# The first x of a batched matmul: eight-row transfers for three of its row tiles, plain transfers for the fourth

## The chip, the cores and the metric

The kernel runs on one core of a Trainium2 chip. The core has five engines that run at their own pace: TensorE (PE) multiplies and transposes, VectorE (DVE) and ScalarE (ACT) copy results out of PE's accumulators, GpSimd (POOL) and SyncE (SP) here only issue transfers. Sixteen DMA engines move data between the chip's memory (HBM) and the core's on-chip memory (SBUF, 128 partitions). Each issuing engine has its own queue to these sixteen: the profile calls POOL's queue q0 and SP's q1.

The metric is device time in microseconds (us); it was 514.31 as the median of three runs (514.30 to 514.31). A profile of one further execution shows what every engine and every DMA packet did.

## The reference

```python
batch, m, k, n = 32, 512, 1024, 768
"x": np.random.randn(batch, m, k).astype(np.float32)
"weight": np.random.randn(batch, k, n).astype(np.float32)

def reference(x, weight):
    return np.matmul(x, weight).astype(np.float32)
```

These are 32 independent products of 512x1024 by 1024x768. All inputs and outputs are 32-bit floats in HBM: 67 MB of x, 101 MB of weights, 50 MB of results.

## The kernel before

Each batch is cut into four row tiles of 128 rows (MT = 4) and eight slices of the contraction (KT = 8). Row tile mt holds the rows 4p + mt of x, p being the partition, so that a partition's four rows lie side by side in HBM, 16 KB in all.

**Loads.** Weights come a batch at a time (`load_w`, line 70), x two batches at a time (`load_pair`, line 60), both from POOL's queue, which turns 32-bit floats into bf16 on the way. Four weight buffers (w_pool) and three x buffers (x_pool) are in use; a load waits on POOL until PE has finished with the buffer that it takes. POOL works its list strictly in order: the weights of batch 0, the identity matrix for the transposes, x of batches 1 and 2, weights 1 and 2, x of 3 and 4, then in the loop weights three batches ahead, x four batches ahead and the stores of finished pairs (`store`, line 164), except the last ones.

**The first x** is the exception. It is loaded by SP as 32-bit floats, which needs no conversion: three of its row tiles go to `x_first` (line 151: one transfer of 128 partitions with 12 KB each) and the fourth to `x_fourth` (line 154: 17 transfers). These 17 are 32, 16, 16, 2 and 2 rows of 4 KB, and then twelve of five rows each, rows of every fourth partition within blocks of twenty. SP keeps eight transfers under way, so each further one waits until an earlier one has landed. SP's list ends with the last stores (lines 182, 184, 185 and 215).

**Compute.** PE must have x with the contraction on the partitions, so it transposes each row tile against an identity matrix, into PSUM (`pt`), and DVE copies it to `xT` in bf16. Line 105 does this for the first x (`transpose_first`), line 78 for the others. The matmuls of line 123 add up eight slices into three accumulators (`pm`) for two row tiles at a time; ACT and DVE copy them to `outs` (lines 143 to 145). For batch 0 three row tiles are transposed before the first matmul, and the fourth when its turn comes (line 211).

**Order.** The program is written in a manual schedule: each engine does its instructions in the order of the source. For batch 0 PE's order is: 24 transposes of `x_first`, the 48 matmuls of the first three row tiles, 8 transposes of `x_fourth`, its 16 matmuls, and then the transposes of batches 1 and 2.

Of the kernel before, what the change touches and what calls it, by code (L numbers as in the profile page):

```python
# [13 lines left out]
def kernel(  # L14
# [6 lines left out]
    nc = tc.nc  # L21
    B, M, K = x.shape
    _, _, N = weight.shape
    P = 128
    MT = M // P
# [21 lines left out]
    x_view = x.rearrange("b (mi mo) k -> b mi mo k", mi=P)  # L47
# [6 lines left out]
    def banks():  # L54
        return [mpsum.tile([P, 512], F32, name=f"pm{i}") for i in range(3)]

    def load_pair(b):

        xs[b] = x_pool.tile([P, 2 * MT, K], BF16, name="x_sb")
        nc.gpsimd.dma_start(out=xs[b], in_=pair_view[b // 2])  # L60

    def load_last():
        xs[B - 1] = x_pool.tile([P, MT, K], BF16, name="x_sb")
        nc.gpsimd.dma_start(out=xs[B - 1], in_=x_view[B - 1])  # L64

    def load_w(b):
        ws[b] = w_pool.tile([P, KT, N], BF16, name="w_sb")
        at = 0
        for n in CHUNKED.get(b, (KT,)):
            nc.gpsimd.dma_start(out=ws[b][:, at:at + n, :], in_=w_view[b, :, at:at + n, :])  # L70
            at += n
# [9 lines left out]
    def transpose_pair(b, mt):  # L81

        both = xT_pool.tile([P, 2, JT, P // 2, 2, 2], BF16, name="xT")
        for half in range(2):
            nc.vector.tensor_copy(  # L85
                both[:, :, :, :, half, :].rearrange("p b j i r -> p j b i r"),
                words(b, mt + MT * half).rearrange("p j (b i r) -> p j b i r", b=2, r=2),
            )
        return [both[:, r].rearrange("p j i h r -> p j (i h) r") for r in range(2)]

    def transpose_last(mt):
        xT = xT_pool.tile([P, JT, P, 2], BF16, name="xT")
        nc.vector.tensor_copy(  # L93
            xT.rearrange("p j m r -> p (j m r)"), words(B - 1, mt).rearrange("p j m -> p (j m)")
        )
        return xT

    def transpose_first(mt):

        xT = xT_pool.tile([P, JT, P, 2], BF16, name="xT")  # L100
        rows = x_first[:, mt] if mt < MT - 1 else x_fourth[:, 0]
        for h in range(2):
            pt = tpsum.tile([P, JT, P], F32, name="pt")
            for i in range(JT):
                nc.tensor.transpose(pt[:, i, :], rows[:, JT * h + i::KT], ident)  # L105
            nc.vector.tensor_copy(  # L106
                xT[:, 2 * h:2 * h + 2].rearrange("p j m r -> p j r m"),
                pt.rearrange("p (j r) m -> p j r m", r=2),
            )
        return xT  # L110
# [8 lines left out]
    def matmuls(pm, half, xT, b, kos, together):  # L119
        for ko in kos:  # L120
            for i, (bank, at, off, size) in enumerate(SPLITS[half]):
                shares = half == 1 and i == 0
                nc.tensor.matmul(  # L123
                    pm[bank][:, at:at + size],
                    xT[:, ko // 2, :, ko % 2],
                    ws[b][:, ko, off:off + size],
                    start=(ko == 0 and not (together and shares)),
                    stop=(ko == KT - 1),
                    skip_group_check=together,
                )  # L130

    def open_out(b):

        if b == B - 2:
            outs[b] = one_pool.tile([P, MT * N], F32, name="one_sb")
            return
        if b % 2 == 0 or b == B - 1:
            twos[b // 2] = out_pool.tile([P, 2, MT * N], F32, name="out_sb")
        outs[b] = twos[b // 2][:, b % 2]

    def evacuate(b, pair, pm):
        o = outs[b][:, pair * N2:(pair + 1) * N2]
        nc.scalar.copy(o[:, 0:512], pm[0])  # L143
        nc.vector.tensor_copy(o[:, 512:1024], pm[1])  # L144
        nc.scalar.copy(o[:, 1024:N2], pm[2])  # L145

    with tc.manual_schedule():

        x_first = x_pool.tile([P, MT - 1, K], F32, name="x_sb")
        x_fourth = one_pool.tile([P, 1, K], F32, name="one_sb")  # L150
        nc.sync.dma_start(x_first, x_view[0, :, :MT - 1])  # L151
        few = [slice(at, first + 20, 4) for first in (0, 20, 40) for at in range(first, first + 4)]
        for rows in (slice(64, 96), slice(96, 112), slice(112, P), slice(60, 62), slice(62, 64), *few):
            nc.sync.dma_start(x_fourth[rows, 0], x_view[0, rows, MT - 1])
        load_w(0)
        ident = const.tile([P, P], F32)
        make_identity(nc, ident)
        load_pair(1)
        load_w(1)
        load_w(2)  # L160
        load_pair(3)

        def store(at):
            nc.gpsimd.dma_start(out=two_view[at], in_=twos[at])  # L164

        ready = {}
        for b in range(B):
            if b % 2 and b + AHEAD + 1 < B:
                if b + AHEAD + 1 == B - 1:
                    load_last()  # L170
                else:
                    load_pair(b + AHEAD + 1)
            if b % 2 and 2 < b < B - HELD - AHEAD:
                store((b - 3) // 2)
            if b + AHEAD < B:
                load_w(b + AHEAD)
            if b == B - LATE:
                store(b // 2 - 2)
                store(b // 2 - 1)
            if b == B - 1:  # L180
                halves = [slice(pair * N2, (pair + 1) * N2) for pair in range(2)]
                nc.sync.dma_start(out_view[b - 1, :, halves[0]], outs[b - 1][:, halves[0]])
                for late in range(B - LATE, B - 2):
                    nc.sync.dma_start(out_view[late], outs[late])
                nc.sync.dma_start(out_view[b - 1, :, halves[1]], outs[b - 1][:, halves[1]])
            open_out(b)
            if b == 0:
                xT = {mt: transpose_first(mt) for mt in range(MT - 1)}
            elif b == B - 1:
                xT = {mt: transpose_last(mt) for mt in range(MT)}  # L190
            else:
                if b % 2:
                    for mt in range(MT):
                        ready[b, mt], ready[b + 1, mt] = transpose_pair(b, mt)
                xT = {mt: ready.pop((b, mt)) for mt in range(MT)}
            if b in CHUNKED:
                pms = [banks() for _ in range(2)]
                at = 0
                for n in CHUNKED[b]:
                    for mt in range(MT):  # L200
                        matmuls(pms[mt // 2], mt % 2, xT[mt], b, range(at, at + n), True)
                        if at + n == KT and mt % 2 == 1:
                            evacuate(b, mt // 2, pms[mt // 2])
                    at += n
                continue
            for pair in range(2):
                pm = banks()
                for half in range(2):
                    mt = 2 * pair + half
                    if mt not in xT:  # L210
                        xT[mt] = transpose_first(mt)
                    matmuls(pm, half, xT[mt], b, range(KT), False)
                evacuate(b, pair, pm)
                if b == B - 1:
                    nc.sync.dma_start(out_view[b, :, halves[pair]], outs[b][:, halves[pair]])
# [30 lines left out]
```

## Time and profile before

| | us |
|---|---|
| median of three runs | 514.31 |
| span of the profiled execution | 512.6 |
| PE busy (84%) | 431.9 |
| DVE busy (25%) | 130.0 |
| ACT busy (15%) | 76.2 |
| PE's first transpose starts (line 105, first three row tiles) | 10.22 |
| PE's first transpose of the fourth row tile | 42.90 |
| first matmul of batch 0 (line 123) | 15.87 |
| last store issued by SP (line 215) | 503.43 |

All times within the execution are counted from its first instruction. The profile's page gives, for each engine, its busy time; the busy share of 40 equal slices of the span as tenths; the DMA queues with their packets, megabytes and share of the 16 engines' time; and groups of equal instructions. Another view, busy time by stretches, gives the same numbers for any stretch of the span. The waits list says which engine stood idle, and whose work ended the wait. Beside these views the trace holds a record of each DMA packet: its queue, start, duration and size. It doesn't name the DMA engine that moved it. A transfer's last packet on each engine is one of 4 bytes, which counts up the semaphore that tells of its landing; so a transfer that is spread over 16 engines leaves 16 of these.

### The profile page before, as it was taken

The page shows a single profiled execution, that of the slowest core. Times are in us where ns is not written, and L with a number is a line of the kernel's source. Part 1 is how long each engine was busy: PE and PEld are TensorE (multiplying, and loading weights), DVE is VectorE, ACT ScalarE, POOL GpSimd, SP SyncE. Part 2 cuts the span into 40 slices and gives each one's busy share as a digit, 9 for nine tenths or more (in the row PEclk, how much of TensorE's full clock was granted, in tenths as well). Part 3 has the DMA queues.
Part 4 walks back from the last instruction along what each step waited for, and adds up shares of the span by engine and source line. Part 5 has one row for each costly group of instructions (what it writes and reads, how often), then busy time and mean ns, then how long its engine had stood idle before and what let it go on. Part 6 is the DMA issues. An engine that isn't in the chain of part 4 may idle for free.

```text
span 512.6 us, 5733 instructions
## 1 busy us (share of the span) xinstructions
PE 431.9 (84%) x2528; PEld 278.5 (54%) x2576; DVE 130.0 (25%) x196; ACT 76.2 (15%) x129; POOL 37.0 (7%) x69
## 2 busy tenths in 40 slices
PE   2806999999999996997979989897897979999992
PEld 1504666666666563664636546464464645666561
DVE  1203223241415140231413204151050410514130
ACT  1100121212121201111111101111111111111210
POOL 3000010101010101001010000101001000010000
PEclk9956999999999998998989979999798997999998
DMA  8999999999999999999999999999999999999998
GB/s 241 223 221 213 218 218 218 333 220 308 245 219 333 217 323 234 226 326 221 328 225 234 318 224 332 217 246 307 221 333 216 258 295 219 331 219 216 322 427 339
DMA packets 12136, 135.63 MB, mean 265 GB/s; under 512 B 1232, under 2 KB 1232, under 8 KB 2128
## 3 DMA queue, kind: packets, MB, share of 16 engines
q0 software_dynamic: 10864, 126.88, 96.5%
q1 hardware_dynamic: 1248, 8.39, 4.1%
q8 instruction: 20, 0.33, 0.2%
q14 instruction: 4, 0.03, 0.0%
HBM read 167.77 MB, written 50.33 MB: 426 GB/s over the span
## 4 chain that ended last, share of the span: by engine, by line
PE 46%; DMA 37%; issue 8%; DVE 5%; another core or an unknown queue 2%; POOL 1%; ACT 0%; SPq 0%; POOLq 0%
PE pm L123 40%; DMA w_sb<-in_weight_dram 29%; DMA one_sb<-in_x_dram 8%; PE pt L78 5%; DVE xT L85 4%; DVE out_sb L144 1%; PE pt L105 0%; POOL out_dram L164 0%; POOL x_sb L60 0%; POOL w_sb L70 0%; DVE one_sb L144 0%; DVE xT L93 0%; ACT out_sb L145 0%; SPq L151 0%
## 5 line engine op out<-in xcount | busy, mean ns | idle before, releaser
L123 PE MATMUL pm<-w_sb,xT 128*128 128x256 bf16 (+1 forms) x2000 | 349.7, 334 | 31.2 <-DMA w_sb<-in_weight_dram 28.7
L123 PEld LDWEIGHTS <-xT 128*128 128x128 bf16 x2048 | 204.6, 100 | 171.8 <-DMA w_sb<-in_weight_dram 32.2
L144 DVE COPY out_sb<-pm 128x512 f32<-128x512 f32 x62 | 42.9, 692 | 318.3 <-PE pm L123 318.3
L78 PE MATMUL pt<-ident,x_sb 128*128 128x128 f32 x496 | 79.8, 303 | 10.4 <-DVE xT L85 10.1
L78 PEld LDWEIGHTS pt<-ident,x_sb 128*128 128x128 f32 x496 | 69.3, 209 | 21.5 <-DVE xT L85 18.7
L85 DVE COPY xT<-pt 128x1024 bf16<-128x1024 bf16 x120 | 77.4, 687 | 11.0 <-PE pt L78 11.0
L143 ACT COPY out_sb<-pm 128x512 f32<-128x512 f32 x62 | 36.3, 585 | 267.4 <-PE pm L123 267.4
L145 ACT COPY out_sb<-pm 128x512 f32<-128x512 f32 x62 | 36.3, 585 | 151.1 <-PE pm L123 151.1
L70 POOL DMA_DIRECT2D w_sb<-in_weight_dram x33 | 18.0, 546 | 406.4 <-PE pm L123 405.6
L105 PE MATMUL pt<-ident,one_sb 128*128 128x128 f32 x8 | 1.9, 422 | 19.0 <-DMA one_sb<-in_x_dram 19.0
L106 DVE CAST xT<-pt 128x512 bf16<-128x512 f32 x8 | 5.9, 732 | 34.8 <-PE pt L105 34.3
L105 PE MATMUL pt<-ident,x_sb 128*128 128x128 f32 x24 | 5.8, 426 | 10.2 <-DMA x_sb<-in_x_dram 10.2
L105 PEld LDWEIGHTS pt<-ident,one_sb 128*128 128x128 f32 x8 | 1.6, 219 | 19.4 <-issue 19.4
L105 PEld LDWEIGHTS pt<-ident,x_sb 128*128 128x128 f32 x24 | 4.4, 214 | 11.2 <-issue 10.2
L164 POOL DMA_DIRECT2D out_dram<-out_sb x14 | 10.1, 719 | 0.4 <-issue 0.3
L60 POOL DMA_DIRECT2D x_sb<-in_x_dram x15 | 8.1, 539 | 11.2 <-PE pt L105 11.2
L144 DVE COPY one_sb<-pm 128x512 f32<-128x512 f32 x2 | 1.4, 692 | 9.0 <-PE pm L123 9.0
L93 DVE COPY xT<-pt 128x1024 bf16<-128x1024 bf16 x4 | 2.6, 686 | 0.2 <-PE pt L78 0.2
L145 ACT COPY one_sb<-pm 128x512 f32<-128x512 f32 x2 | 1.2, 586 | 4.2 <-PE pm L123 4.2
L143 ACT COPY one_sb<-pm 128x512 f32<-128x512 f32 x2 | 1.2, 585 | 3.8 <-PE pm L123 3.8
L143 ACT ACT_TABLE_LOAD x1 | 1.3, 1283 | 0.7 <-PEq L230 0.7
L64 POOL DMA_DIRECT2D x_sb<-in_x_dram x1 | 0.5, 536 | 0.0
(6 smaller groups left out, 0.9 us busy)
## 6 DMA issues: line engine op xcount, KB each, us to landing
w_sb<-in_weight_dram POOLq DMA_DIRECT2D x31, 1536.0 KB, 41.7
out_dram<-out_sb POOLq DMA_DIRECT2D x14, 3072.0 KB, 55.8
x_sb<-in_x_dram POOLq DMA_DIRECT2D x15, 2048.0 KB, 50.2
out_dram<-out_sb SPq DMA_DIRECT2D x2, 1536.0 KB
x_sb<-in_x_dram SPq DMA_DIRECT2D x1, 1536.0 KB
w_sb<-in_weight_dram POOLq DMA_DIRECT2D x2, 768.0 KB, 48.8
out_dram<-one_sb SPq DMA_DIRECT2D x2, 768.0 KB
out_dram<-out_sb SPq DMA_DIRECT2D x2, 768.0 KB
```

What stands on the lines that cost most here:

```text
L60: nc.gpsimd.dma_start(out=xs[b], in_=pair_view[b // 2])
L70: nc.gpsimd.dma_start(out=ws[b][:, at:at + n, :], in_=w_view[b, :, at:at + n, :])
L78: nc.tensor.transpose(pt[:, j, :], pairs[:, mo, j::JT], ident)
L85: nc.vector.tensor_copy(both[:, :, :, :, half, :].rearrange("p b j i r -> p j b i r"), words(b, mt + MT * half).rearrange("p j (b i r) -> ...
L93: nc.vector.tensor_copy(xT.rearrange("p j m r -> p (j m r)"), words(B - 1, mt).rearrange("p j m -> p (j m)"))
L105: nc.tensor.transpose(pt[:, i, :], rows[:, JT * h + i::KT], ident)
L106: nc.vector.tensor_copy(xT[:, 2 * h:2 * h + 2].rearrange("p j m r -> p j r m"), pt.rearrange("p (j r) m -> p j r m", r=2),)
L123: nc.tensor.matmul(pm[bank][:, at:at + size], xT[:, ko // 2, :, ko % 2], ws[b][:, ko, off:off + size], start=(ko == 0 and not (together an ...
L143: nc.scalar.copy(o[:, 0:512], pm[0])
L144: nc.vector.tensor_copy(o[:, 512:1024], pm[1])
L145: nc.scalar.copy(o[:, 1024:N2], pm[2])
L164: nc.gpsimd.dma_start(out=two_view[at], in_=twos[at])
```

## The change

Only the loads of the first x are changed. `x_first` comes in seven transfers: partitions 48 to 127 in one, and the partitions 0 to 47 in six of eight partitions each, every sixth partition. `x_fourth` comes in three transfers of 64, 32 and 32 partitions. The same rows go to the same places. The order on POOL, PE, DVE and ACT is the same as before; on SP 10 loads stand where 18 stood.

```diff
         x_first = x_pool.tile([P, MT - 1, K], F32, name="x_sb")
         x_fourth = one_pool.tile([P, 1, K], F32, name="one_sb")
-        nc.sync.dma_start(x_first, x_view[0, :, :MT - 1])
-        few = [slice(at, first + 20, 4) for first in (0, 20, 40) for at in range(first, first + 4)]
-        for rows in (slice(64, 96), slice(96, 112), slice(112, P), slice(60, 62), slice(62, 64), *few):
+        few = [slice(at, 48, 6) for at in range(6)]
+        for rows in (slice(48, P), *few):
+            nc.sync.dma_start(x_first[rows], x_view[0, rows, :MT - 1])
+        for rows in (slice(0, 64), slice(64, 96), slice(96, P)):
             nc.sync.dma_start(x_fourth[rows, 0], x_view[0, rows, MT - 1])
         load_w(0)
```

Line 151 of the kernel before becomes line 153 (`x_first`), line 154 becomes line 155 (`x_fourth`); the later lines move down by one.

## The prediction

> **What bounds the kernel now.** I read the slices first, then the DMA queues, then busy time by stretches, and the waits last.
>
> ```profile
> DMA  8999999999999999999999999999999999999998
> ...
> q0 software_dynamic: 10864, 126.88, 96.5%
> q1 hardware_dynamic: 1248, 8.39, 4.1%
> q8 instruction: 20, 0.33, 0.2%
> ...
> HBM read 167.77 MB, written 50.33 MB: 426 GB/s over the span
> ```
>
> The mean share of the 16 DMA engines is 90% or more in all but the first and the last slice. POOL's queue (q0) holds 96.5% of that time; SP's (q1), which alone the change touches, 4.1%. q8 matters below: 20 packets that fetch instructions.
>
> ```profile
> 6.00:48.00 42.00, 18.70 (x94) 12.43 (x95) 6.55 (x9) 1.75 (x3) 0.53 (x1) 0.76 1.03 225
> 48.00:170.00 122.00, 117.89 (x724) 78.35 (x737) 38.22 (x58) 21.06 (x36) 9.79 (x17) 1.00 1.02 254
> 170.00:424.00 254.00, 218.64 (x1260) 138.55 (x1283) 64.05 (x97) 38.04 (x65) 20.12 (x35) 0.94 1.02 265
> 424.00:504.00 80.00, 76.66 (x455) 49.17 (x462) 21.18 (x32) 14.05 (x24) 2.48 (x4) 0.97 1.02 297
> 504.00:509.00 5.00, 0.00 (x0) 0.00 (x0) 0.00 (x0) 0.00 (x0) 0.00 (x0) 0.85 0.98 409
> ```
>
> In these stretches PE's busy time stands before the first bracket, and the DMA share is the last number but one. It is 1.02 to 1.03 from 6 to 504 us (packets overlap a little at their seams) and 0.98 until 509: the DMA engines never run dry, however busy PE is. The end belongs to them too: the last store is issued at 503.43 and the last packet ends at 511.18.
>
> ```profile
> PE pt L105 <- DMA one_sb<-in_x_dram: 19.0, 1, 19.0
> ...
> PE pm L123 <- DMA w_sb<-in_weight_dram: 28.7, 9, 5.5
> ```
>
> PE waits 19.0 us at the head for the fourth row tile and 28.7 us later for weights. The chain of waits calls PE 46% of the span, but an engine that starts 19 us late and later waits 28.7 us has not set the pace. So the question is which of the 16 DMA engines has the most to do.
>
> **How far apart the engines run.** The records of the packets show it: each transfer on q0 ends in 16 packets of 4 bytes, one an engine. Their times for three transfers:
>
> ```
> x of batches 3, 4    48.38-48.91 (11 engines)   50.45-50.83 (5 engines)
> w of batch 26        420.30 420.44 420.55       421.94 ... 423.32 (13)
> out of batches 24,25 486.35 486.38 486.38       487.83 ... 489.34 (13)
> ```
>
> The five late ones at 50 us carry the twelve five-row transfers of line 154. Two of them are latest, by 2.44 us against the first: they have 14 extra packets with 14 completions, 2.44/14 = 0.174 us a pair. I followed each engine from transfer to transfer by its shift. Eight engines, none of the five, are thrown back by 0.93 to 1.13 us again and again, at the times of the 20 q8 packets, always in the same order of eight: two or three times each before the end. Three engines are neither late nor ever hit: they are the 486.35 to 486.38 above and end at 508.39, while the last ends at 511.18. The five stand at 488.03 to 488.63 by then, the eight at 487.84 to 489.34; the mean of all is 488.04. So perfect balance would be worth 489.34 - 488.04 = 1.30 us, and no more.
>
> **The change part by part.** SP's list goes from 18 loads to 10. Bytes are the same, 512 rows of 4 KB. In the records a 12 KB packet follows the one before it after 0.441 us (460 ns less 19 overlapped), a 4 KB one after 0.153.
>
> Which engines: the trace has 128, 32 and 16 rows on sixteen engines, five rows on five, two on two of these five. So I put 80 rows on sixteen (five each) and eight rows on eight, the five and three more. The other bound for the 80 is fewer engines, which I take up as a rival.
>
> - An engine outside the eight: three packets of 12 KB fewer, four of 4 KB more (eight plain rows against four): -3 x 0.441 + 4 x 0.153 = -0.71 us.
> - One of the eight: the same plus six packets of 12 KB with a completion of 0.022 each: -0.71 + 6 x 0.463 = +2.07 us against a plain engine before. The two with 14 extra pairs lose those: 2.07 - 2.44 = -0.37. The three with 12: 2.07 - 12 x 0.174 = -0.02. The three newcomers: +2.07.
> - Idle at the head: an engine outside the eight has done its five packets at about 5.2 us (the 80th packet of the trace started at 4.85), and q0's first packet starts at 5.84. In between only the fourth tile can fill it, which SP issues seventh. SP's issues take 0.25 to 0.77 us each, so it arrives 1.03 us (0.74 to 1.77, as the first load) after 3.1 to 6.2. Idle is 0 to 0.7 us; I take 0.2, as the 0.38 to 0.46 of most issues puts it at about 4.8.
> - The three newcomers are either the three that are never hit, or among the eight that are. I take the first: the five are spared as well, so five and three would be one block of eight, beside the block of eight that takes the refills in turn. No row numbers the engines; the other choice is the rival below.
>
> [...]
>
> [...] The trace's five-row transfers do fall on five engines only.
>
> Then, at the 486 to 489 us transfer: newcomers 486.38 + 2.07 = 488.45; the five at most 488.63 - 0.02 = 488.61; the eight that are hit at most 489.34 - 0.71 + 0.2 = 488.83. The last engine is 489.34 - 488.83 = 0.51 us earlier. Engines drift by up to 0.4 us from causes I can't place (the three unhit ones moved 0.65 to 1.13 over the run without a fetch), and with sixteen now close together the latest of them is more likely to be unlucky: I take 0.1 off. Sum: -0.4 us. The profiled span is 512.6 us, the median 514.31, so 1.7 lie around it and stay: 514.31 - 0.4 = 513.9.
>
> **What moves and costs nothing.** The first three tiles land later. Line 105 now starts at 10.22. On the eight, q0 and q1 take turns from 5.84 us on, one packet each, completions too, as the records show. About seven of eleven packets have started by then; three are left with four completions between seven weight packets of 0.907: 6.1 + 7 x 0.907 + 3 x 0.455 = 13.9 us. The fourth tile's eight rows and three completions then take 11 turns, mostly beside x packets of 1.208: about 26.7 us against 42.7 now, where two waits stand in SP's list and not ten. PE: 14.0 + 5.84 + 8.0 = 27.8, no wait, + 1.94 + 3.67: batch 0 done at about 33.5 instead of 48.3. PE is 15 us early, and that buys nothing: one pair of batches takes PE 26.47 us and the DMA engines 31.55 (170.67 to 423.70, eight periods), so the 15 us come back as longer waits for weights, from about 100 us on instead of 170. What hides PE is this surplus of DMA work; if it were gone, PE's tail would show whole. What waits behind the later start is POOL's load at line 60, now at 16.36, then at about 20; q0 has work until 58 by then.
>
> **Rivals.**
> The slower side: the newcomers are refill engines. Speaks for it: eleven engines are outside the five, eight of them hit. Against: the five are all spared, which a random draw of eight from sixteen seldom does. Price: 487.84 to 489.34 + 2.07 = 489.91 to 491.41, so the last is 0.6 to 2.1 us later; with three newcomers the worst is likely near the top: +1.8, 516.1. It decides once a newcomer's last transfer comes later than 489.34, from its first refills on.
>
> PE's head counts: if PE set the end, 15 us would go: about 499.5. For it: the chain's 46% PE and 19.0 us. Against: the DMA share of 1.02 through both stages, and 5.7 us from the last store's issue to the landing of a store that q1 could do alone in 8 x 0.234 = 1.9.
>
> The transfers don't spread as read: 80 rows on five engines would be 16 packets each there, 11 x 0.441 = 4.9 us more than five, on engines that take the eights as well: about 519. Nothing speaks for it but that 80 is in no row.
>
> **Numbers.** The forecast 0.66, refill engines 0.29, PE's head 0.02, no spread 0.03. About 0.2% (1.03 us) is what a measurement of this kernel tells from no change. The forecast's own range is 513.2 to 514.7; 0.12 of its chance lies beyond 1.03 us faster, where drift would have to help balance it nearly wholly. 0.05 of the refill case stays within 0.2%. Faster 0.12 + 0.02 = 0.14; same 0.54 + 0.05 = 0.59; slower 0.24 + 0.03 = 0.27. The range, 513.2 to 516.3, takes in the refill case up to 2.0 us.
>
> **What would show it.** Line 105's first matmul near 14 us, its wait for the fourth tile near nothing; the first wait for weights near 100 us, their sum near 28.7 + 15 = 44; DMA share still 1.02; the x transfer of batches 3 and 4 with eight engines 2.8 us behind eight; in the last transfers no early group of three. The forecast is wrong if three of the late eight are thrown back by fetches, if a DMA stretch falls under 1, or if the first packet of q0 moves.

## The result and the profile after

| | before | after |
|---|---|---|
| median of the runs of this comparison | 514.33 us (514.30 to 514.46, 8 runs) | 515.68 us (515.21 to 516.61, 8 runs) |
| ratio, 95% interval | | 1.0028 (1.0019 to 1.0037) |
| profiled execution, and its span | 514.3, 512.6 | 516.61, 514.8 |
| last DMA packet ends | 511.18 | 513.52 |

The change makes the kernel 1.35 us slower, where the forecast was 0.4 faster; to "slower" the prediction had given 0.27. The eight times fall in two groups, 515.21 to 515.76 and 516.42 to 516.61; the profile shows an execution of the upper one. The steps below are therefore read from an execution 0.9 us above the median.

From the page, the slices, the queues and the traffic of after:

```profile
DMA  8999999999999999999999999999999999999996
...
q0 software_dynamic: 10864, 126.88, 96.0%
q1 hardware_dynamic: 1232, 8.39, 4.2%
q8 instruction: 20, 0.33, 0.2%
...
HBM read 167.77 MB, written 50.33 MB: 424 GB/s over the span
```

Same bytes, sixteen completions fewer on q1 (1232 packets for 1248), and a last slice at 6 tenths instead of 8: fewer engines are at work at the end. From busy time by stretches (stretch, length, PE, PE's weight loads, DVE, ACT, POOL with their counts, granted clock, DMA share, GB/s), the first row of before and then rows of after:

```profile
0.00:6.00 6.00, 0.00 (x0) 0.00 (x0) 0.00 (x0) 1.28 (x1) 4.03 (x12) 1.00 0.71 229
```

```profile
0.00:6.00 6.00, 0.00 (x0) 0.00 (x0) 0.00 (x0) 1.28 (x1) 4.04 (x12) 1.00 0.75 186
6.00:48.00 42.00, 26.49 (x158) 18.68 (x161) 12.22 (x18) 2.94 (x5) 1.07 (x2) 1.00 1.02 229
48.00:170.00 122.00, 111.76 (x662) 71.69 (x672) 33.07 (x50) 20.54 (x35) 10.66 (x19) 0.97 1.02 254
170.00:424.00 254.00, 222.52 (x1256) 140.19 (x1280) 63.35 (x96) 37.57 (x64) 18.42 (x33) 0.93 1.02 266
424.00:504.00 80.00, 74.55 (x455) 48.35 (x464) 21.19 (x32) 14.09 (x24) 2.89 (x5) 1.00 1.01 296
...
509.00:514.80 5.80, 0.00 (x0) 0.00 (x0) 0.00 (x0) 0.00 (x0) 0.00 (x0) 0.50 0.27 112
```

PE is busy 26.49 us between 6 and 48 us, against 18.70. Yet the DMA share in the long stretches is 1.02 and 1.01, as before, so the end is still the DMA engines'. In the first 6 us the engines are busy for 0.75 and move 186 GB/s, where before they were busy for 0.71 and moved 229: more time for fewer bytes. From the timeline of after, SP's first issues and PE's head (start, length, what, count, idle before and who ended it):

```profile
0.74 4.57 SPq L153 DMA_DIRECT2D x_sb<-in_x_dram  x7
5.36 3.61 SPq L155 DMA_DIRECT2D one_sb<-in_x_dram  x3
```

```profile
20.20 4.57 PE L105 MATMUL pt<-ident,x_sb 128*128 128x128 f32 x20 [20.20 <-DMA x_sb<-in_x_dram]
...
25.47 7.96 PE L123 MATMUL pm<-w_sb,xT 128*128 128x512 bf16 x47
33.27 1.05 PE L105 MATMUL pt<-ident,one_sb 128*128 128x128 f32 x8
34.70 2.77 PE L123 MATMUL pm<-w_sb,xT 128*128 128x256 bf16 x16 [0.37 <-DVE xT L106]
37.31 1.11 PE L78 MATMUL pt<-ident,x_sb 128*128 128x128 f32 x8
```

PE starts at 20.20, not at 10.22; the fourth tile follows without a wait, and batch 0 is done at 37.3 where it was 48.3. From the waits of after (total us, times, longest):

```profile
PE pm L123 <- DMA w_sb<-in_weight_dram: 34.0, 12, 4.2
...
PE pt L105 <- DMA x_sb<-in_x_dram: 20.2, 1, 20.2
```

The 19.0 us for the fourth tile are gone, 20.2 stand ahead of the first, and the weights' waits grow from 28.7 to 34.0. PE's 11 us came back as waits and as busy time, which is 435.3 in all against 431.9.

The packets say where the end moved. The completions of the same transfers as before, one an engine, in after:

```
x of batches 3, 4     48.34 48.36 48.38 48.42 48.44 | 49.10 49.42 50.24 | 50.87 50.92 51.04 51.04 51.16 51.16 51.20 51.35
                      mean 49.96 (before: 49.31)
out of batches 24,25  485.24 485.95 487.43 ... 490.30 490.91 492.55     mean 488.53 (before: 488.04, latest 489.34)
ends of last stores   ... 511.48 511.55 511.67 511.87 | 513.19 513.52   (before: ... 511.18)
```

Eight engines carry the six extra transfers: 50.87 to 51.35, some 2.7 us behind the five earliest. Of the three in between, one has been thrown back by a refill (a q8 packet, which fetches instructions) at 39 us; what delayed the others is open. Followed by its shifts, one of the eight (51.04) is thrown back by 1.09 us at the instruction refills of 79, 278 and 473 us, another (51.20) at those of 100, 303 and 495. These two are the 513.19 and 513.52 at the end, 1.3 and 1.6 us behind all others. Two engines that are never thrown back are outside the eight, and finish early. The 492.55 overstates the distance: SP's stores are issued from 485.42 us on and run beside this transfer, and at the one before it, the weights of batch 31, the latest engine stands at 483.84, 2.05 us later than in before (481.79).

On average the engines are late from the start: the mean at 50 us is 0.65 up, although the five earliest stand where before's earliest do. The 128 packets of `x_first` took 83.6 us together (mean 0.653 each) instead of 73.8 (0.577): 9.8 / 16 = 0.62 an engine. The slow ones are those of the 80-row transfer: the 79 that start in the first 6 us take 60.3 us together, 0.76 each; before's 108 in the same time took 64.3, 0.60 each. This lead of before doesn't keep its size: at the weights of batch 31 the mean is 480.99 against 480.67, 0.32 up, and why is open.

### The profile page after: what moved, and what is told of

It is laid out like the page before. It is cut to its first block, busy times and chain, and to the rows that moved or that the text cites. A ratio compares the mean times of both kernels' runs of the same rounds, so it can differ in the third digit from the quotient of the medians.

```text
span 514.8 us, 5725 instructions
## 1 busy us (share of the span) xinstructions
PE 435.3 (85%) x2528; PEld 278.9 (54%) x2576; DVE 129.8 (25%) x196; ACT 76.4 (15%) x129; POOL 37.1 (7%) x69
## 3 DMA queue, kind: packets, MB, share of 16 engines
q1 hardware_dynamic: 1232, 8.39, 4.2%
## 4 chain that ended last, share of the span: by engine, by line
PE 44%; DMA 41%; issue 5%; DVE 4%; another core or an unknown queue 2%; SPq 1%; POOL 1%; ACT 0%; POOLq 0%
PE pm L123 38%; DMA w_sb<-in_weight_dram 38%; PE pt L78 4%; DMA x_sb<-in_x_dram 3%; DVE xT L85 3%; PE pt L105 1%; DVE out_sb L144 1%; SPq L153 1%; DVE xT L106 0%; POOL out_dram L165 0%; POOL x_sb L60 0%; POOL w_sb L70 0%; DVE one_sb L144 0%; DVE xT L93 0%
## 5 line engine op out<-in xcount | busy, mean ns | idle before, releaser
L123 PE MATMUL pm<-w_sb,xT 128*128 128x256 bf16 (+1 forms) x2000 | 354.8, 337 | 36.9 <-DMA w_sb<-in_weight_dram 34.0
L105 PE MATMUL pt<-ident,x_sb 128*128 128x128 f32 x24 | 5.3, 385 | 20.4 <-DMA x_sb<-in_x_dram 20.2
L105 PEld LDWEIGHTS pt<-ident,x_sb 128*128 128x128 f32 x24 | 4.1, 210 | 21.4 <-issue 20.2
```

Source lines behind the costliest of these rows:

```text
L123: nc.tensor.matmul(pm[bank][:, at:at + size], xT[:, ko // 2, :, ko % 2], ws[b][:, ko, off:off + size], start=(ko == 0 and not (together an ...
```

## Experiments

Three theories stood for the 1.35 us. T: two of the eight are refill engines (engines that refills throw back; the others are called spared), and they finish last. S: the packets of the 80-row transfer are slow, and delay every engine. H: PE's first tiles come too late (20.2 for 10.2). All runs lie beside runs of the kernel before on the same chip, in three groups.

| | median (range, runs) | before, same chip | ratio (95%) |
|---|---|---|---|
| e1_plain | 516.46 (516.32 to 517.0, 5) | 514.58 | 1.0036 (1.0024 to 1.0048) |
| e2_middle | 516.66 (516.39 to 518.16, 5) | 514.58 | 1.0045 (1.0033 to 1.0057) |
| e3_six | 517.99 (517.17 to 518.4, 5) | 514.58 | 1.006 (1.0048 to 1.0072) |
| e4_fourth_six | 515.55 (514.91 to 516.87, 12) | 514.58 | 1.0015 (1.0005 to 1.0025) |
| e5_fourth_eight | 515.08 (514.73 to 515.88, 11) | 514.60 | 1.0011 (1.0002 to 1.002) |
| e6_eighty | 518.79 (518.67 to 520.57, 5) | 514.60 | 1.0088 (1.0074 to 1.0102) |
| e7_late | 526.11 (526.01 to 526.19, 4) | 514.60 | 1.0222 (1.0208 to 1.0236) |
| e8_fourth_five | 514.89 (514.82 to 515.06, 11) | 514.60 | 1.0004 (0.9995 to 1.0013) |
| e9_again | 516.46 (515.54 to 516.97, 6) | 514.75 | 1.0028 (1.0016 to 1.0039) |
| e10_blocks | 524.87 (524.76 to 524.97, 2) | 514.75 | 1.0192 (1.0174 to 1.0211) |
| e11_strides | 517.48 (517.31 to 517.64, 2) | 514.75 | 1.0049 (1.003 to 1.0067) |
| e12_pe_late | 514.51 (514.18 to 515.17, 11) | 514.75 | 0.9994 (0.9985 to 1.0003) |

The kernel before itself ranged from 514.17 to 516.03 in these groups, wider than in the comparison above; differences of a few tenths between kernels of different groups mean nothing.

### The eights undone

```diff
-        few = [slice(at, 48, 6) for at in range(6)]
-        for rows in (slice(48, P), *few):
-            nc.sync.dma_start(x_first[rows], x_view[0, rows, :MT - 1])
+        nc.sync.dma_start(x_first, x_view[0, :, :MT - 1])
```

> The six eight-row transfers are undone: x_first comes in one transfer of 128 partitions as before, x_fourth stays in three plain transfers, so all sixteen engines carry the same 32 rows. Theory T (two of the engines that get the six extra packets also take instruction refills, and finish last): each engine has 4 x 0.153 = 0.61 us more than a plain engine before, refilled ones included, so 514.3 + 0.6 = 514.9, with executions close together. Rival S (the first packets of the 80-partition transfer take 0.84 us instead of 0.46 and hold all engines up): 514.3 to 514.9, packets near 0.46 us again. Rival H (the loss comes from the first tiles landing 10 us later): the first transpose is back near 10 us, so 514.3 or less.

516.46: T's number is missed by 1.6 us, and S and H are missed as well, since the head is quick again. The timeline of e1, PE:

```profile
10.26 5.84 PE L105 MATMUL pt<-ident,x_sb 128*128 128x128 f32 x24 [10.26 <-DMA x_sb<-in_x_dram]
...
23.92 1.05 PE L105 MATMUL pt<-ident,one_sb 128*128 128x128 f32 x8
```

PE starts at 10.26 and has the fourth tile at 23.92 without a wait, the earliest of all kernels here; the packets of `x_first` have a median of 473 ns; and it is slower than before. The completions show who is late: fourteen engines stand together at 49.03 to 49.58 at x of batches 3 and 4, and at the transfer of batches 24 and 25 the unhit ones are at 486.23 to 487.39, the hit ones at 488.28 to 491.74. With nothing extra on the engines that are spared, two refilled ones end alone, at 512.86 and 513.07. So taking out the five-row transfers of before, with nothing in their place, cost 1.9 us. Of this T explains what a refill costs; a further 2 us by which the engines hit three times fell back, largely in steps of 0.1 to 0.4, it doesn't. What makes these steps stays open, and they may be at work in the changed kernel too.

### The eights in the middle, and six instead of eight

```diff
-        few = [slice(at, 48, 6) for at in range(6)]
-        for rows in (slice(48, P), *few):
+        few = [slice(at, end, 3) for end in (24, P) for at in range(end - 24, end - 21)]
+        for rows in (slice(24, 104), *few):
```

> As the changed kernel, but the 80 plain partitions of x_first are 24 to 103 (40 in each half of the SBUF partitions) and the eights take 0 to 23 and 104 to 127. The same bytes on the same number of engines. Theory T: the two engines still carry both loads; only the slow start's 0.4 to 0.6 us goes, so 515.1 to 515.3, executions still up to 1.4 us apart. Rival S: the whole loss goes with the slow first packets, 514.3 or less. Rival H: the first transpose still starts at 18 to 20 us, so 515.7 as the changed kernel. If partitions don't set the pace of the first packets, these stay at 0.84 us and the time at 515.7.

516.66, later than every number put on it, and no cure: the packets' median is 676 ns (after: 559), the mean at x of batches 3 and 4 50.56. Where the 80 partitions lie is not what makes them slow, or not in this simple way.

```diff
-        few = [slice(at, 48, 6) for at in range(6)]
+        few = [slice(at, 48, 8) for at in range(8)]
```

> As the changed kernel, but the 48 partitions come in eight transfers of six rows instead of six of eight, so six engines get eight extra packets and the two disputed ones none. Theory T: no late engine is refilled; the six are at 488.6 - 2.1 - 0.7 + 8 x 0.463 + 0.4 (slow start) = 489.9 in the transfer where the last stood at 489.34 before, so 514.3 + 0.6 = 514.9, and executions within 0.3 us. Rival S: start as slow as in the changed kernel, 515.7. Rival H: the first tiles land later still (16 turns instead of 12), 515.7 or more.

517.99: T's number is missed by 3 us, and how these divide between two hits of one late engine and the slow start is open. Six engines are late now, with eight extra packets each (52.13 to 52.78 against 48.20 to 49.43), and one of the six, at 52.60, is thrown back by refills at 177 and 382 us. The latest completion at the transfer of batches 24 and 25 is 492.50, the last packet 513.84. So one of the six is no spared one. If the five of before are among them, it is the engine that a six-row transfer takes beyond these five; it is called the sixth below.

### The spread alone, on the fourth tile

These three leave `x_first` as before, so the head is not disturbed, and spread the fourth tile's rows over six, eight and five engines.

```diff
+        nc.sync.dma_start(x_first, x_view[0, :, :MT - 1])
+        few = [slice(at, 96, 16) for at in range(16)]
+        for rows in (slice(96, P), *few):
             nc.sync.dma_start(x_fourth[rows, 0], x_view[0, rows, MT - 1])
```

> The kernel before with another spread of the fourth tile: 32 rows plain and 96 in sixteen transfers of six rows. Theory T: six engines that are never refilled get 16 extra pairs of 0.174 us (2.8 us), the others two rows fewer (-0.31): refilled engines at 489.34 - 0.31 = 489.03, the six at 488.0 to 489.0, so 514.3 - 0.3 = 514.0, executions within 0.2 us. If a sixth engine is refilled (the boundary lies at five), 489.34 + 2.5, so up to 516.8. Rivals S and H: nothing at the head changes for the better (the fourth tile lands later, near 48 us), 514.3 or more.

515.55, in two groups, 514.91 to 515.16 and 515.93 to 516.87. T's own number, 514.0, is missed; its other branch, a refilled sixth engine, had up to 516.8. In the profile (516.75) six engines are late at x of batches 3 and 4: 50.72, 50.77, 50.82, 50.88, 50.93 and 51.92. The last is one already thrown back, at 48 us; it is thrown back again at 225 and 430. At the transfer of batches 24 and 25 the latest is at 492.57 and the next at 489.11, and the last packet ends at 513.68, 1.85 us behind the next (511.83). Five of the six are spared, the sixth is a refill engine.

```diff
+        few = [slice(at, 112, 14) for at in range(14)]
+        for rows in (slice(112, P), *few):
```

> The kernel before with x_first in one transfer and the extra rows in the fourth tile on eight engines: 16 rows plain and 112 in fourteen transfers of eight. The eight carry 14 extra pairs of 0.174 us (2.44), the others three rows fewer (-0.46); the head is not slowed (first transpose near 10.2 us). Theory T: two of the eight are refilled; the one that stood at 488.65 before with three refills now stands at 488.65 - 0.46 + 2.44 = 490.6 and sets the end 1.3 us later, with two refills 0.2 later: 514.5 to 515.6, in two clusters about 1.1 us apart. Rivals S (slow first packets) and H (late first tiles): neither is there, so 514.3 or less.

515.08, in two groups 0.9 us apart where T had 1.1: 514.73 to 515.08 and 515.79 to 515.88. The waits and the timeline of e5:

```profile
PE pt L105 <- DMA one_sb<-in_x_dram: 14.7, 1, 14.7
...
PE pt L105 <- DMA x_sb<-in_x_dram: 10.6, 1, 10.6
```

```profile
10.60 5.43 PE L105 MATMUL pt<-ident,x_sb 128*128 128x128 f32 x24 [10.60 <-DMA x_sb<-in_x_dram]
...
38.52 1.95 PE L105 MATMUL pt<-ident,one_sb 128*128 128x128 f32 x8 [14.70 <-DMA one_sb<-in_x_dram]
```

The head is that of before, with the fourth tile 4 us earlier; the packets of `x_first` take 473 ns in the median; the mean at x of batches 3 and 4 is 49.40. Only the spread is left of the change: eight late engines, 50.25 to 51.45, of which two are thrown back three times (46, 224, 429 us and 65, 255, 451). These two end at 512.65 and 512.70, all others by 510.85. This is T alone, in a profile of the upper group: 1.8 us behind the rest, and 1.5 behind the end of before.

```diff
+        few = [slice(at, 80, 16) for at in range(16)]
+        for rows in (slice(80, 112), slice(112, P), *few):
```

> The kernel before with four more five-row transfers: 48 rows of the fourth tile plain, 80 in sixteen transfers of five. The five engines that take no refills get 16 extra pairs (2.78 us) instead of 12 or 14, the others three rows instead of four. Theory T: refilled engines 0.15 us earlier (489.19), the five at 488.6 to 489.2, so 514.33 - 0.15 = 514.2, no cluster 1 us higher than the kernel before has beside it. Rivals S and H: unchanged, 514.3.

514.89: no difference from before, and no two groups. The five late engines are never thrown back, and the last packet ends at 511.35. T's small gain is not there, but its boundary is: five engines cost nothing, six and eight do, with small transfers of one 4 KB row an engine in all three, and with PE's first tile at 10.2 to 10.6 us in all three.

### The 80-row transfer without the eights

```diff
-        few = [slice(at, 48, 6) for at in range(6)]
-        for rows in (slice(48, P), *few):
+        for rows in (slice(48, P), slice(0, 48)):
```

> No eights at all, but x_first in two plain transfers, partitions 48 to 127 and 0 to 47; the fourth tile plain as in the changed kernel. Beside the run with one transfer of 128 (e1_plain, 516.46) this tells what the 80-partition transfer alone costs. Rival S: its packets take 0.84 us again, so 0.4 to 0.6 us more than that run, 516.9 to 517.1. If the slow first packets come from the eights instead: 516.4, packets near 0.47. Theory T takes no side here; on its count of the refilled engines the time is as in that run plus what the start loses.

518.79, 2.3 us more than e1, which differs in this line alone: two transfers of 80 and 48 rows in place of one of 128. S has the direction, and about a fifth of the size: it had 0.4 to 0.6 us more than e1. The stretch to 6 us, first of e6, then of e1:

```profile
0.00:6.00 6.00, 0.00 (x0) 0.00 (x0) 0.00 (x0) 1.28 (x1) 4.03 (x12) 1.00 0.70 174
```

```profile
0.00:6.00 6.00, 0.00 (x0) 0.00 (x0) 0.00 (x0) 1.28 (x1) 4.03 (x12) 1.00 0.69 225
```

The engines are busy for the same share, 0.70 and 0.69, and move 174 instead of 225 GB/s. A 12 KB packet takes 836 ns in the median, not 473, and the mean at x of batches 3 and 4 is 52.15 instead of 49.47: of the 2.7 us lost at the head, 2.3 are there at the end.

### Which rows are moved together

```diff
-        for rows in (slice(48, P), *few):
+        for rows in [slice(at, at + 16) for at in range(0, P, 16)]:
```

> Measures the slow first packets: x_first in eight transfers of 16 neighbouring partitions each, one row an engine, the fourth tile plain. All engines carry the same. [...] If the slowness is HBM's (rows 16 KB apart), they take what the next run's take or less; if only 80 or 48 partitions in one transfer are slow, 0.46.

```diff
-        for rows in (slice(48, P), *few):
+        for rows in [slice(at, P, 8) for at in range(8)]:
```

> [...]

Both have eight transfers of sixteen partitions on sixteen engines, one packet an engine, and differ only in which partitions go together: neighbours in e10, every eighth one in e11. The stretch to 6 us of e10, then of e11:

```profile
0.00:6.00 6.00, 0.00 (x0) 0.00 (x0) 0.00 (x0) 1.28 (x1) 4.02 (x12) 1.00 0.74 123
```

```profile
0.00:6.00 6.00, 0.00 (x0) 0.00 (x0) 0.00 (x0) 1.28 (x1) 4.03 (x12) 1.00 0.70 152
```

Packets take 1158 ns in the median and 1753 at most in e10, 488 and 828 in e11. e10 ends at 524.87, its mean at x of batches 3 and 4 is 57.82. e11's is 49.89: its packets are quick, but by 8 us the engines have worked 3.8 engine-us less than before's, 0.24 an engine. So how long a packet takes depends on which rows are moved at one time. Whether the partitions that they go to decide it, or the places in HBM that they come from, these runs can't tell, since both change together: neighbours lie 16 KB apart in HBM, every eighth row 128 KB. The longest packets settle nothing, for the one transfer of 128 rows has packets of up to 1540 ns in before and 1789 in e1, and the medians lie well below (473 ns in e1). Why the packets are slow, here or in the 80-row transfer, is not shown: e2, with its 80 partitions in the middle, was not better (676 ns in the median, after: 559).

### A late head alone

```diff
+        nc.sync.dma_start(x_first, x_view[0, :, :MT - 1])
         load_w(0)
```

(The same line is taken out ahead of before's seventeen transfers of the fourth tile, so that the first three tiles come last.)

> The kernel before with SP's list turned round: the 17 transfers of the fourth tile first, then the one of x_first. The same transfers on the same engines, but the first three tiles land at 40 us or later instead of 10, so that PE starts 30 us later or more. Rival H (the late first tiles are what costs): far more than the 1.35 us of the changed kernel, which delayed them by 10 us; 517 or more. Theory T: the load of each engine is unchanged and the DMA engines have work without a gap, so 514.3 to 514.8, and PE's waits for weights shrink. It could fall apart on both if q0 runs dry, as POOL's load of batches 5 and 6 then waits for x_first's buffer until 50 us.

526.11, and no verdict on H at 20 us: PE starts at 46.5, far later than in after, and the loads stall. Busy time by stretches of e7:

```profile
48.00:75.00 27.00, 25.79 (x160) 17.64 (x159) 12.51 (x19) 3.40 (x6) 1.06 (x2) 1.00 0.97 203
75.00:170.00 95.00, 92.98 (x580) 60.51 (x578) 25.83 (x40) 17.58 (x31) 8.90 (x16) 1.00 0.95 246
```

The DMA share falls to 0.97 and 0.95, where the other kernels have 1.01 to 1.02: POOL's load at line 60 waits 46.9 us for PE's transposes (11.2 in before), and the DMA engines run dry. This is the price of a late head; with the next run, it begins somewhere between 17 and 46 us.

```diff
             if b == 0:
+                for _ in range(10):
+                    pt = tpsum.tile([P, JT, P], F32, name="pt")
+                    for i in range(JT):
+                        nc.tensor.transpose(pt[:, i, :], x_first[:, 0, i::KT], ident)
                 xT = ...
```

(Added to the kernel before, ahead of its first transposes; the results of these 40 are not used.)

> The kernel before with 40 more transposes on PE ahead of its first (their results are not used), which delay the first row tiles by 10 us on PE and POOL's load behind them to 26 us, as in the changed kernel, with no transfer changed. Rival H: 1.35 us slower, 515.7. Theory T: the engines' loads are the same, so as the kernel before on the same chip, within 0.3.

514.51, ratio 0.9994 (0.9985 to 1.0003). The timeline of e12, PE:

```profile
10.21 7.07 PE L191 MATMUL pt<-ident,x_sb 128*128 128x128 f32 x40 [10.21 <-DMA x_sb<-in_x_dram]
17.11 1.04 PE L105 MATMUL pt<-ident,x_sb 128*128 128x128 f32 x8
...
42.95 1.95 PE L105 MATMUL pt<-ident,one_sb 128*128 128x128 f32 x8 [13.75 <-DMA one_sb<-in_x_dram]
```

The first tiles are transposed 6.9 us later than before, at 17.11, and POOL's load at line 60 goes out at 21.70 instead of 16.36. Nothing is lost. The delay is short of after's 10, so H is refuted for 7 us and, with a DMA share of 1.02 in after where e7 has 0.95, unlikely for 10.

### The changed kernel again

No edit: one more profile of the changed kernel.

> The changed kernel once more, for a second profile and its clusters. Theory T: executions fall in two clusters about 1 us apart, by whether the two refilled engines among the eight are hit two or three times; in the profile the two engines that finish last are late at 50 us and are hit by refills. If the profile falls in the lower cluster, the two are hit twice at most before 489 us and the last packet ends about 1 us earlier than 513.5. Rivals S and H have no reason for clusters.

516.46 in six runs (515.54 and 515.73, then 516.40 to 516.97), the profile again of the upper group. The same picture: the engines hit at 79, 278 and 473 and at 100, 303 and 496 us end at 513.29 and 513.36, the next at 512.06; the mean at x of batches 3 and 4 is 50.16, the packets' mean 693 ns. What sets the two groups apart may be whether such an engine is hit two or three times: the profiles of after, e4, e5 and e9 are of upper groups and show three hits, that of e3 is of its lower group (517.27; the others are 517.17 and 517.99 to 518.4) and shows two, and a hit is worth about the distance. No lower execution of the changed kernel was profiled: argued, not shown.

## Why the prediction failed

**The step that failed** is "the three newcomers are either the three that are never hit, or among the eight that are. I take the first". Two of the three are refill engines: the sixth (e4) and one of the seventh and eighth (e5 and after; which of them is open). The reason given, that five spared engines and three spared newcomers would be one block of eight, was symmetry and not a row. The rival on the slower side was what happened; its point of decision, a newcomer later than 489.34 at the transfer of batches 24 and 25, was passed by 3.2 us (492.55; some 1.2 of the 3.2 arose in this transfer itself, beside SP's stores). Its price, 516.1, lies near the measured 515.68, in part by luck: eight extra-loaded engines with an undisturbed head (e5) cost 0.48 us in the median and 1.25 in the upper group, and the rest of the 1.35 has other sources, which the rival did not contain. The range, 513.2 to 516.3, holds the result because it takes in this rival, and not because the forecast's own sum did.

**Mis-sized, on the same side: the head.** Idle of 0.2 us was put there. The engines hardly idled (by 8 us they had worked 94.1 engine-us, before's 94.9) but worked slowly: the mean at x of batches 3 and 4 is 0.65 us later, 0.62 of it slow packets of the 80-row transfer, whose duration had been taken from the 128-row one. That they cost time at the end is shown by e6, where the packets of `x_first` take 105.8 us together and the end is 2.3 us later; how much of the 0.65 is left at the end of the changed kernel is not settled. The last packet apart from the two refilled engines ends 0.69 after before's (511.87 against 511.18), but the mean at the weights of batch 31 is only 0.32 later. The two engines end 1.65 us after that packet in the profiled execution; the median of all runs, 1.35 up, holds less of this than the profile does.

**Right: what bounds the kernel.** The DMA share stayed at 1.02, and PE's head, 11 us earlier, bought nothing; e1 had batch 0 done 9 us earlier still and was slower than before, e12 later and equal. The extra load was sized well: eight engines 2.7 us behind the five earliest, against 2.07 + 0.71 = 2.78, though three others stand in between. The first wait for weights came at 108 us (about 100), the fourth tile without a wait.

**Mis-sized without effect on the end.** `x_first` landed at 20.2, not 13.9. Seven of eleven packets were to be done when q0 began; in fact SP needed 4.57 us for its seven issues, 0.65 each, and by 6.0 us only 79 packets had started, fewer than the 80-row transfer alone has. The "0.38 to 0.46 of most issues" was a misreading; the issues of the fourth tile in before (shortest, median and longest in ns) were

```profile
L154 SPq DMA_DIRECT2D one_sb<-in_x_dram x17: 248/657/772, 1.2 to 28.4; - x17
```

On the eight engines all twelve turns were still to come: 5.8 + 12 x 0.907 + 6 x 0.56 = 20.0. Batch 0 was done at 37.3, not 33.5, so the waits for weights grew to 34.0 and not 44, PE's busy time taking 3.4 of the rest.

**Slips that move nothing.** The sum given as 13.9 is 13.8. Eight periods from 170.67 to 423.70 are 31.63 us each, not 31.55. From the last store's issue (503.43) to the last packet's end (511.18) it is 7.75 us and not 5.7, which speaks against PE's head the more. The fourth tile is SP's eighth load, not its seventh. Of the signs of being wrong, the first came with two engines of the late eight instead of three; the DMA share of the long stretches stayed at 1.01 or above, and q0's first packet moved by 0.36 us (from 5.84 to 5.48).

**Not confirmed.** "Perfect balance would be worth 1.30 us" was read from before's completions, and the loss of 0.1 for drift was a guess. e1, plain everywhere, was to be 514.9 by the same bookkeeping and was 516.46. Where its three-hit engines lose 2 us more than their refills is not known, so the bookkeeping by shifts is good to about 1.5 us and not to the 0.1 that the sum was written in.

## What to carry to other kernels

In after the sixteen DMA engines were busy all along (a share of 1.01 to 1.02 from 6 to 504 us), and the end was that of the two with the most to do, 1.3 and 1.6 us behind all others. Small transfers served here as weights on chosen engines: with five engines weighted the ratio to before was 1.0004 (e8), with none 1.0036 (e1), with six 1.0015 (e4). To use them so, first find out, from the completions of a plain kernel and the times of the instruction refills, which engines are thrown back anyway, and stop at the boundary that the trace shows (five here). When a transfer is cut by partitions, other rows are moved at one time: cut in two, the first x had packets of 836 ns in the median against 473 (e6 and e1), so the duration of the uncut transfer was no estimate for it. When a prediction needs an identity that no row gives (which engine, which buffer), price both and say that it is a coin toss, instead of letting symmetry decide.

## What the hardware showed that was not expected

- The engines that take the 20 instruction refills of an execution come in a fixed order of eight. Two of the refill packets, of 878 to 894 ns against 921 to 975 for the others, stand next to each other in it, and in after, e4, e5 and e9 they are the ones that hit engines inside the spread: the first of the two is the sixth engine. No wait of PE in the waits list is put down to a refill, but the DMA engine that carries one is 0.93 to 1.13 us late from then on, and that decided this case.
- A 12 KB packet of the first x took 0.47 us in the median of one load (e1) and 1.16 in another (e10), by which rows were moved beside it.
- SP's issues of the eight-row loads take 0.62 to 0.77 us each, so the last of the six is issued at 4.69 us, 4 us after the first load of all.
- Executions of one kernel on one chip fell in two groups about 1 us apart (after, e4, e5; in e5 514.73 to 515.08 and 515.79 to 515.88), where no group is seen with five engines (e8, 514.82 to 515.06).
